# Attention logits on all 128 rows of TensorE, and forget-gate bias tiles by broadcast DMA

## The chip, the cores and the metric

The kernel runs on one core of a Trainium2 chip. A core has five engines with instruction streams of their own: TensorE (PE in the rows of the profile; its weight loads are PEld), VectorE (DVE), ScalarE (ACT), GpSimd (POOL) and SyncE (SP), which here only issues DMAs. The metric is the device time of one execution in microseconds, lower is better; the median of three runs is given.

## The reference

Two transformer blocks in float32, over 1024 tokens of width 1024. Block 1 has a token mixer with 16 heads of 64 (8 heads with a forget gate, 8 with a band of earlier chunks) and a convolutional feed-forward; block 2 has gated linear attention and a squared-relu feed-forward. The change touches only the logits of block 1's two kinds of attention:

```python
# forget heads: cum = running sum of log f
logits = einsum('bhqd,bhkd->bhqk', qb, k) * d**-0.5        # d = 64
logits = logits + cb[..., :, None] - cum[..., None, :]
logits = where(k_pos <= q_pos, logits, -inf)
# band heads: own chunk of 64 and the 8 chunks before it
logits = einsum('bhcqd,bhckd->bhcqk', qc, k_band) * d**-0.5 + bias
p = softmax(logits);  out = p @ v
```

The part of the forget bias that is the same for a whole row of queries, `cb`, cancels in the softmax, so the kernel adds one value per key.

## The kernel before

A float32 value is held as two `float32r` parts, a rounded high one and the rest, low. A product of two such numbers is the sum of high x high, high x low and low x high, accumulated in one PSUM bank; `mm3` (lines 130 to 132) does that in three matmuls with 128 contracted rows.

A head has 64 features, so the high and the low part of one head's queries fit into the 128 rows together. For each pair of heads `k_out` and `q_out` write, from the PSUM result of the projection: `X0`, with the high part of head 0's queries in rows 0 to 63 and the low part (with the other sign) in rows 64 to 127; `X1`, the same for head 1 with the halves exchanged; `Y0` and `Y1`, the keys with the parts the other way round, so that one matmul over 128 rows gives high x low plus low x high; and `Dk`, the high parts of the keys of both heads, 64 rows each. `stage_qk` then takes two matmuls for a strip of up to 512 keys: line 373 with `X` and `Y` on 128 rows, and line 375 with the 64 rows of `X` and `Dk` that hold the high parts. In the forget heads a third one (line 377, bf16) puts the causal mask on the last 128 columns. VectorE adds the bias tile and takes the row's extreme (line 378), ScalarE the exponential (381), VectorE the reciprocal (382), GpSimd the scaling (383). TensorE transposes the result (line 90, `ptp`), it is split in two parts (`ph` on ScalarE, `pl` on VectorE), and line 427 multiplies them with the values.

The bias tile of a forget head (heads 8 to 15) is made by `make_bias`: two matmuls (line 343) with 64 rows of the running sums `cums` against a selector, and two copies by ScalarE (line 344). The bias of a band head comes by DMA (line 346) and is changed by GpSimd.

The attention phase merges several streams: the attention itself (logits run AHEAD = 3 query tiles before the rest), the projections of the next pair of heads or of the values, the modulation products `ada` (loads of `ada_w` on SP, sums on GpSimd), and near the end the loading of earlier results. A scheduler then fixes the order on every engine before the kernel runs; each engine works strictly in that order, and SP issues its DMAs in order too, each one waiting for its source and for its destination to be free. Pairs of heads have their `X` and `Y` tiles in two buffers, logits have two PSUM banks (`S`), bias tiles two buffers.

Of the kernel before, what the change touches and what calls it, by code (L numbers as in the profile page):

```python
# [14 lines left out]
ALU = mybir.AluOpType  # L15
# [28 lines left out]
def merge(gens):  # L44
    """Interleaves streams by their shares of tensor-engine time: gens is a list of (gen, total)."""
    live = [[g, float(total), 0.0] for g, total in gens]
    while live:
        s = min(live, key=lambda e: e[2] / e[1])
        try:
            s[2] += next(s[0]) or 1.0  # L50
        except StopIteration:
            live.remove(s)


def build(tc, I, out, dbg=None, stop=None):
# [13 lines left out]
    def set_banks(st, n, plan):  # L69
        """PSUM of a phase: tag -> (bank count of a tile, buffers, purposes)."""  # L70
        banks.clear()
        for tag, (width, bufs, uses) in plan.items():
            pl = pool(st, f"ps{n}{tag}", bufs, space=PSUM)
            for u in uses.split():
                banks.setdefault(u, deque()).append((pl, tag, 512 * width))
# [6 lines left out]
    def exp_tables(after):  # L82
        """ScalarE's set with both Exp and Ln, once no other one is wanted."""
        with tc.issue_after(after.ins):
            ACT.preload_act_table_set("natural_log_exp_and_others")

# [28 lines left out]
    def w_get(ap, n=P):  # L115
        """Weights loaded and split, in two pieces: the parts of each row block of n columns."""
        m = ap.shape[-1] // 2
        out = []
        for i in range(2):
            r = rawp.tile([P, m], F32, tag="raw", name="raw")  # L120
            SP.dma_start(out=r, in_=ap[:, i * m:i * m + m])
            h = wp.tile([P, m], F32R, tag="wh", name="wh")
            l = wp.tile([P, m], F32R, tag="wl", name="wl")
            split(r, h, l)
            out += [(h[:, c:c + n], l[:, c:c + n]) for c in range(0, m, n)]
        return out

    def mm3(o, ah, al, bh, bl, first, last):
        """o += a^T b of operands in parts: all products but the one below float32's last bit."""
        PE.matmul(out=o, lhsT=ah, rhs=bh, start=first, stop=False)  # L130
        PE.matmul(out=o, lhsT=ah, rhs=bl, start=False, stop=False)  # L131
        PE.matmul(out=o, lhsT=al, rhs=bh, start=False, stop=last)  # L132
# [11 lines left out]
    def ada(v, c0, n, ar, ac):  # L144
        """Columns c0 to c0 + n of modulation vector v: products with the columns of ada_w, summed over rows by VectorE, over partitions by TensorE."""
# [37 lines left out]
    # =====================================================================  # L183
    # block 1: the token mixer
    # =====================================================================
    ydram = [tc.dram_tile([P, T], F32, name=f"ydram{p}") for p in range(8 if stop == "attn" else 7)]

    def attention_phase():
# [25 lines left out]
        def k_out(p, half, psum):  # L214
            Y0, Y1, Dk = pair[p][2:]
            c = slice(half * 512, half * 512 + 512)
            a, b = slice(0, 64), slice(64, 128)
            ACT.copy(Dk[:, c], psum)
            ACT.copy(Y0[b, c], psum[a])
            ACT.copy(Y1[a, c], psum[b])  # L220
            DVE.tensor_tensor(out=Y0[a, c], in0=psum[a], in1=Dk[a, c], op=ALU.subtract)
            DVE.tensor_tensor(out=Y1[b, c], in0=psum[b], in1=Dk[b, c], op=ALU.subtract)

        def alloc_pair(p):
            pair[p] = [qkp.tile([P, T], F32R, tag=n, name=n) for n in ("X0", "X1", "Y0", "Y1", "Dk")]
# [38 lines left out]
        def weights(n, half):  # L264
            """Half of the first pair's weights, in the place of the values to come."""
            r = rawp.tile([P, 512], F32, tag="raw", name="raw")
            h, l = (vp.tile([P, 512], F32R, tag=f"v{4 * n + 2 * half + i}", name="w0") for i in range(2))
            SP.dma_start(out=r, in_=Wqk[n][:, half * 512:half * 512 + 512])
            split(r, h, l)
            wqk[n].append((h, l))  # L270
# [30 lines left out]
        sel8 = f1.tile([64, 8], F32R, name="sel8")  # L301
        selt = f1.tile([64, 8], F32, name="selt")
        DVE.tensor_copy(out=selt, in_=ident[0:64, 0:8])
        DVE.tensor_copy(out=selt[32:64], in_=ident[32:64, 32:40])
        DVE.tensor_copy(out=sel8, in_=selt)
# [5 lines left out]
        cums = f1.tile([64, T], F32R, name="cums")  # L311

        def forget_sums():
            """The forget gates' running sums, in parts."""
            fa = pp.tile([P, T], F32, tag="P", name="fa")[0:8]
            fb = pp.tile([P, T], F32, tag="P", name="fb")[0:8]
            POOL.memset(cums.bitcast(F32), 0.0)
# [13 lines left out]
            ACT.copy(cums[0:8], fa)  # L331
            DVE.tensor_tensor(out=cums[32:40], in0=fa, in1=cums[0:8], op=ALU.subtract)

# [1 line left out]
        bias = {}  # L335

        def make_bias(h):
            bt = bp.tile([P, T], F32, tag="bias", name="bias")
            if h >= 8:
                for half in range(2):  # L340
                    c = slice(half * 512, half * 512 + 512)
                    psum = acc("S")
                    PE.matmul(out=psum, lhsT=sel8[:, h - 8:h - 7].to_broadcast([64, P]), rhs=cums[:, c], start=True, stop=True)
                    ACT.copy(bt[:, c], psum)
# [13 lines left out]
        def stage_qk(h, j, i):  # L358
            t = 2 * j + i
            X0, X1, Y0, Y1, Dk = pair[h // 2]  # L360
            X, Y = (X0, Y0) if h % 2 == 0 else (X1, Y1)
            rows = slice(0, 64) if h % 2 == 0 else slice(64, 128)
# [7 lines left out]
            for n, (c0, c1) in enumerate(zip(cuts, cuts[1:])):  # L370
# [4 lines left out]
                PE.matmul(out=S, lhsT=X[rows, tq], rhs=Dk[rows, kc], start=False, stop=not diag)  # L375
# [89 lines left out]
        def ahead(n):  # L465
            """The logits of the first n query tiles; a negative yield before those of a new pair."""
# [108 lines left out]
    def rstd_of(v, eps, scale=1.0):  # L575
        """(scale * v + eps) ** -0.5 for [P, 1]."""
# [8 lines left out]
    def layer_norm(r, mv, g, b, junk, eng=None):  # L585
        """r: a row's values; mv[:, 0:2]: the sums of its halves."""
# [7 lines left out]
    def add_sum(o, a, b, s):  # L594
        """o = a + b, s its sum over the row."""
        DVE.tensor_tensor_reduce(out=o, in0=a, in1=b, scale=1.0, scalar=0.0, op0=ALU.add, op1=ALU.add, accum_out=s)  # L596
# [6 lines left out]
    def transposed(src, t, hi_t=None, lo_t=None, full=None, scale=None, shift=None, use="xtp"):  # L603
        """[128 tokens, 1024] -> columns of the split transposed activations, with a scale and a shift by feature."""
# [25 lines left out]
    def square_product(wname, wo, done, scale=None, ks=range(KD)):  # L630
        """tokens x 1024 = (transposed activations)^T @ weights, by halves of the columns and token tiles."""
# [35 lines left out]
    def low_rank(hs, ht, c0, n):  # L667
        """[tokens, 32] of n tokens -> their columns of the gates' right factor, in parts."""
# [8 lines left out]
    def gates(hs, h, c0, n, e, with_q):  # L677
        """Per direction, of one head and n tokens: decays to and from the middle of each 128-token tile, and over its two chunks."""
# [35 lines left out]
    def tile_factors(e, nt):  # L714
        """The factor from one tile's state to the next one's, in the order of the direction."""
# [26 lines left out]
    def k_tokens(kts, bufs=None):  # L742
        """[dk, 128 tokens] each -> [128 tokens, dk] side by side."""
# [8 lines left out]
    def context(st):  # L752
        """The states that the context leaves, by head and direction."""
# [21 lines left out]
        def states(h, ek, v, e):  # L775
            """The two directions' states: the keys of the two tiles with the decays that follow them, times the values."""
            kts = []
            for d in range(2):
                a = d
                # the decay over the last chunks, and from the first tile to the second, by direction  # L780
# [80 lines left out]
    # =====================================================================  # L861
    # block 1: the convolutional feed-forward; block 2's modulation beside it
    # =====================================================================
# [40 lines left out]
    def ffn():  # L904
# [57 lines left out]
        def first_values():  # L962
            """The first head's values, and the gates' low-rank products."""
# [58 lines left out]
    # =====================================================================  # L1022
    # block 2: gated linear attention
    # =====================================================================
# [39 lines left out]
    def scan(h):  # L1064
# [17 lines left out]
        def step(d, t, s, tag):  # L1082
            """The state entering the next tile of this direction, with that tile's first decay."""
# [82 lines left out]
    # =====================================================================  # L1166
    # block 2: the squared-relu feed-forward
    # =====================================================================
# [58 lines left out]
def tiles_of(w, cols):  # L1227
    """[d, cols] with d = k * 128 + p as rows p of (k, col)."""
# [11 lines left out]
def by_part(v):  # L1240
    """A vector of 1024 features as [128, 8]."""
# [3 lines left out]
def cut(w):  # L1245
    """[n * 128, 1024] as [n, 2, 128, 512]."""
# [70 lines left out]
```

## Time and profile before

| | before |
|---|---|
| median of 3 runs | 2671.27 us (2670.43 to 2673.04) |
| profiled execution: span from first to last instruction | 2669.8 us; no time of its own beside the span is listed |
| mean granted TensorE clock | 0.993 |
| busy over the span: TensorE, VectorE, ScalarE, GpSimd | 98%, 52%, 38%, 17% |
| attention phase, where the change lies | about 35 to 567 us of the span |
| DMA | 184.93 MB, mean 69 GB/s |

Ends of matmuls are modelled, so a busy TensorE is not one at its peak: how fast it goes is read from the distance between the starts of neighbouring matmuls. In rows of the timeline, two numbers stand first, the start and the duration in us, then the engine, the line, the operation with output<-inputs, rows*columns of the array that are active, and the shape of the moving operand. A bracket at the end says how long the engine idled before and what ended it; "issue" means nothing that the profile shows.

### The profile page before, as it was taken

Reading aid. Unit: us, or ns where it says so; the run is one execution under the profiler, and the core shown is the slowest. Engines: PE = TensorE matmul, PEld = TensorE weight load, DVE = VectorE, ACT = ScalarE, POOL = GpSimd, SP = SyncE. Lnnn points to the kernel's source line nnn. Section 1 sums busy time; section 2 is a strip of 40 time slices with the busy share of each in tenths; the row PEclk is TensorE's granted clock in tenths of the full one; section 3 lists DMA queues with packets and bytes.
Section 4 is the critical chain, followed back from the end, with each engine's and each line's share of the span. In section 5 each row is a group of like instructions: output and inputs, shape, how many; then the busy total and the mean of one; then the engine's idle time right before and its main releaser. Section 6 shows DMA issues by size and latency. Waiting matters only on the chain.

```text
span 2669.8 us, 35397 instructions
## 1 busy us (share of the span) xinstructions
PE 2619.0 (98%) x13322; PEld 2187.1 (82%) x13322; DVE 1396.4 (52%) x2681; ACT 1011.3 (38%) x1909; POOL 445.2 (17%) x598
## 2 busy tenths in 40 slices
PE   8999999999999999999999899999999999999998
PEld 7787877778878888888887788899878888888887
DVE  5756556466755554554556766434442333333365
ACT  5555555564532222222224744333263222222223
POOL 4565632333200000000003400000020000000031
PEclk9999999999999999999999999999999999999999
DMA  4222110142322222222221210102331111111122
GB/s 152 71 61 71 46 51 23 57 156 72 108 86 71 89 63 73 82 64 70 91 79 65 72 38 22 41 28 96 117 104 48 51 48 48 48 48 48 48 83 79
DMA packets 113819, 184.93 MB, mean 69 GB/s; under 512 B 13936, under 2 KB 46320, under 8 KB 113648
## 3 DMA queue, kind: packets, MB, share of 16 engines
q1 hardware_dynamic: 113648, 182.68, 21.5%
q8 instruction: 104, 1.70, 0.3%
q14 instruction: 67, 0.55, 0.1%
HBM read 164.28 MB, written 18.35 MB: 68 GB/s over the span
## 4 chain that ended last, share of the span: by engine, by line
PE 63%; issue 30%; POOL 3%; DVE 2%; ACT 1%; DMA 1%; POOLq 0%; DVEq 0%; SPq 0%; ACTq 0%
PE down L130 4%; PE down L131 4%; PE down L132 4%; PE up L131 4%; PE up L130 4%; PE up L132 4%; PE proj L130 3%; PE proj L132 3%; PE proj L131 3%; PE y L427 3%; PE S L375 2%; PE ptp L90 2%; PE tokp L131 2%; PE tokp L130 2%; PE tokp L132 2%
## 5 line engine op out<-in xcount | busy, mean ns | idle before, releaser
L130 PE MATMUL up<-act_hi,wh 128*128 128x512 f32 x1216 | 475.2, 391 | 6.8 <-DVE conv L922 2.5
L131 PE MATMUL up<-act_lo,wh 128*128 128x512 f32 x1216 | 475.9, 391 | 0.2 <-DVE act_lo L624 0.2
L132 PE MATMUL up<-act_hi,wl 128*128 128x512 f32 x1216 | 474.5, 390 | 0.0
L102 ACT CAST wh<-raw 128x512 fp32r<-128x512 f32 (+2 forms) x268 | 166.3, 624 | 554.7 <-PE up L131 501.2
L103 DVE TENSOR_TENSOR wl<-raw,wh 128x512 fp32r<-128x512 f32 (+2 forms) x268 | 202.4, 761 | 281.4 <-ACT wh L102 268.6
L130 PE MATMUL down<-wdh,gh 128*128 128x512 f32 x864 | 337.6, 391 | 1.1 <-DVE mv L596 0.7
L131 PE MATMUL down<-wdl,gh 128*128 128x512 f32 x864 | 336.9, 390 | 0.3 <-DVE wdl L103 0.2
L132 PE MATMUL down<-wdh,gl 128*128 128x512 f32 x864 | 331.5, 390 | 0.2 <-DVE gl L103 0.2
L130 PEld LDWEIGHTS up<-act_hi,wh 128*128 128x128 f32 x1216 | 228.6, 188 | 55.5 <-ACT conv L920 2.9
L131 PEld LDWEIGHTS up<-act_lo,wh 128*128 128x128 f32 x1216 | 228.8, 188 | 48.0 <-DVE act_lo L624 1.0
L132 PEld LDWEIGHTS up<-act_hi,wl 128*128 128x128 f32 x1216 | 228.8, 188 | 47.3
L579 POOL TENSOR_TENSOR rstd<-rstd,mhalf 128x1 f32<-128x1 f32 x74 | 49.8, 673 | 1241.9 <-DVE rstd L578 1226.6
L102 ACT CAST wdh<-wdraw 128x512 fp32r<-128x512 f32 x108 | 67.1, 622 | 378.6 <-PE down L132 283.3
L1191 DVE TENSOR_TENSOR res<-res,down 128x512 f32<-128x512 f32 x160 | 107.3, 686 | 171.9 <-PE down L132 171.6
L130 PEld LDWEIGHTS down<-wdh,gh 128*128 128x128 f32 x864 | 162.3, 188 | 36.8 <-DVE mv L596 2.2
L131 PEld LDWEIGHTS down<-wdl,gh 128*128 128x128 f32 x864 | 162.3, 188 | 34.5 <-DVE wdl L103 1.3
L132 PEld LDWEIGHTS down<-wdh,gl 128*128 128x128 f32 x864 | 162.2, 188 | 34.2 <-DVE gl L103 0.6
L130 PE MATMUL tokp<-wh,act_hi 128*128 128x256 f32 (+1 forms) x512 | 150.2, 295 | 0.0
L131 PE MATMUL tokp<-wl,act_hi 128*128 128x256 f32 (+1 forms) x512 | 149.7, 293 | 0.0
L132 PE MATMUL tokp<-wh,act_lo 128*128 128x256 f32 (+1 forms) x512 | 148.6, 291 | 0.0
L383 POOL TENSOR_SCALAR P<-P,mx 128x640 f32<-128x640 f32 (+7 forms) x128 | 96.7, 757 | 255.1 <-DVE mx L382 210.5
L381 ACT ACTIVATE P<-P,mx 128x640 f32<-128x640 f32 (+7 forms) x128 | 94.5, 738 | 96.2 <-DVE mx L378 88.5
(302 smaller groups left out, 5205.5 us busy)
## 6 DMA issues: line engine op xcount, KB each, us to landing
ada_w<-in_ada_w SPq DMA_DIRECT2D x192, 128.0 KB, 2.1
raw<-in_w_up SPq DMA_DIRECT2D x88, 256.0 KB, 2.6
raw<-in_mlp_w SPq DMA_DIRECT2D x64, 256.0 KB, 2.6
wdraw<-in_mlp_w SPq DMA_DIRECT2D x64, 256.0 KB, 2.8
wdraw<-in_w_down SPq DMA_DIRECT2D x44, 256.0 KB, 2.6
raw<-in_wqk SPq DMA_DIRECT2D x32, 256.0 KB, 2.8
raw<-in_g_qk SPq DMA_DIRECT2D x24, 256.0 KB, 2.6
raw<-in_g_v SPq DMA_DIRECT2D x24, 256.0 KB, 2.7
```

The lines of the kernel that those rows point to most:

```text
L90: PE.transpose(out=o, in_=a, identity=ident)
L102: ACT.copy(h, raw)
L103: DVE.tensor_tensor(out=l, in0=raw, in1=h, op=ALU.subtract)
L130: PE.matmul(out=o, lhsT=ah, rhs=bh, start=first, stop=False)
L131: PE.matmul(out=o, lhsT=ah, rhs=bl, start=False, stop=False)
L132: PE.matmul(out=o, lhsT=al, rhs=bh, start=False, stop=last)
L375: PE.matmul(out=S, lhsT=X[rows, tq], rhs=Dk[rows, kc], start=False, stop=not diag)
L381: ACT.activation(Pm[:, 0:W], Pm[:, 0:W], AF.Exp, bias=mx[:, 0:1], scale=-1.0, accum_out=mx[:, 1:2])
L383: POOL.tensor_scalar(out=Pm[:, 0:W], in0=Pm[:, 0:W], scalar1=mx[:, 2:3], scalar2=0.0, op0=ALU.mult, op1=ALU.add)
L427: PE.matmul(out=o, lhsT=lhsT, rhs=part[:, off:off + w], start=(first and n == 0 and m == 0), stop=(last and n == len(cur) - 1 and m == 1))
L579: POOL.tensor_tensor(out=t[:, 1:2], in0=t[:, 0:1], in1=mhalf, op=ALU.pow)
L1191: DVE.tensor_tensor(out=r, in0=r, in1=psum, op=ALU.add)
```

## The change

The 64-row matmul with `Dk` becomes one with 128 rows. `Dk` goes, and each head gets a tile `Z` with its keys' high part where `X` has the queries' high part, and the low part where `X` has the low one. So `X` with `Z` gives high x high plus low x low. ScalarE writes the high parts and VectorE the low parts only into the half of the rows where the PSUM result has them; four DMAs for each half of the columns copy them to the other half of the rows, into the other tile (`Y` from `Z`, `Z` from `Y`; 64 rows of 512 values, 128 KB, each). For the bias, the running sums are stored to memory once (`cumd`), and the bias tile of a forget head is one DMA that reads one row of it for all 128 partitions (512 KB); the selector, `cums`, the 16 matmuls and 16 copies go.

```diff
 def k_out(p, half, psum):
-    Y0, Y1, Dk = pair[p][2:]
+    Y0, Y1, Z0, Z1 = pair[p][2:]
     ...
-    ACT.copy(Dk[:, c], psum)
-    ACT.copy(Y0[b, c], psum[a])
-    ACT.copy(Y1[a, c], psum[b])
-    DVE.tensor_tensor(out=Y0[a, c], in0=psum[a], in1=Dk[a, c], op=ALU.subtract)
-    DVE.tensor_tensor(out=Y1[b, c], in0=psum[b], in1=Dk[b, c], op=ALU.subtract)
+    ACT.copy(Z0[a, c], psum[a])
+    ACT.copy(Z1[b, c], psum[b])
+    DVE.tensor_tensor(out=Y0[a, c], in0=psum[a], in1=Z0[a, c], op=ALU.subtract)
+    DVE.tensor_tensor(out=Y1[b, c], in0=psum[b], in1=Z1[b, c], op=ALU.subtract)
+    for o, i, to, of in ((Y0, Z0, b, a), (Y1, Z1, a, b), (Z0, Y0, b, a), (Z1, Y1, a, b)):
+        SP.dma_start(out=o[to, c].bitcast(F32), in_=i[of, c].bitcast(F32))
 ...
-    cums = f1.tile([64, T], F32R, name="cums")
+    cumd = tc.dram_tile([8, T], F32, name="cumd")
 def forget_sums():
-    POOL.memset(cums.bitcast(F32), 0.0)
     ...
-    ACT.copy(cums[0:8], fa)
-    DVE.tensor_tensor(out=cums[32:40], in0=fa, in1=cums[0:8], op=ALU.subtract)
+    SP.dma_start(out=cumd, in_=fa)
 def make_bias(h):
     if h >= 8:
-        for half in range(2):
-            c = slice(half * 512, half * 512 + 512)
-            psum = acc("S")
-            PE.matmul(out=psum, lhsT=sel8[:, h - 8:h - 7].to_broadcast([64, P]), rhs=cums[:, c], start=True, stop=True)
-            ACT.copy(bt[:, c], psum)
+        SP.dma_start(out=bt, in_=cumd[h - 8:h - 7, :].to_broadcast([P, T]))
 def stage_qk(h, j, i):
-    X0, X1, Y0, Y1, Dk = pair[h // 2]
-    X, Y = (X0, Y0) if h % 2 == 0 else (X1, Y1)
-    rows = slice(0, 64) if h % 2 == 0 else slice(64, 128)
+    X, Y, Z = pair[h // 2][h % 2::2]
     ...
     PE.matmul(out=S, lhsT=X[:, tq], rhs=Y[:, kc], start=True, stop=False)
-    PE.matmul(out=S, lhsT=X[rows, tq], rhs=Dk[rows, kc], start=False, stop=not diag)
+    PE.matmul(out=S, lhsT=X[:, tq], rhs=Z[:, kc], start=False, stop=not diag)
```

The scheduler orders the phase anew. The first place is TensorE where the fourth pair of heads (heads 6 and 7) has its first logits; `S` is their PSUM bank, `proj` are projections, `ptp` transposes, `y` products with the values. Before, with lines 373 and 375:

```order
L427 MATMUL y_2789<-ph_2771,v3_2321 128x128
L427 MATMUL y_2789<-pl_2772,v3_2321 128x128
L90 MATMUL ptp_2947<-ident_67,P_2663 128x128
L373 MATMUL S_2907<-Y0_2595,X0_2593 128x128
L375 MATMUL S_2907<-Dk_2597,X0_2593 128x128
L90 MATMUL ptp_2947<-ident_67,P_2702 128x128
L130 MATMUL proj_2931<-act_hi_71,wh_2921 128x512
```

and in the changed kernel, where the two logit matmuls are lines 361 and 363:

```order
L132 MATMUL proj_2880<-act_hi_71,wl_2822 128x512
L361 MATMUL S_2928<-Y0_2609,X0_2607 128x128
L130 MATMUL proj_2953<-act_hi_71,wh_2943 128x512
L131 MATMUL proj_2953<-act_lo_72,wh_2943 128x512
L132 MATMUL proj_2953<-act_hi_71,wl_2944 128x512
L130 MATMUL proj_2953<-act_hi_71,wh_2943 128x512
L131 MATMUL proj_2953<-act_lo_72,wh_2943 128x512
L363 MATMUL S_2928<-Z0_2611,X0_2607 128x128
L132 MATMUL proj_2953<-act_hi_71,wl_2944 128x512
```

The second matmul of the strip, which reads the later of the two copies, stands five projections behind the first.

The second place is SP while the second pair's keys (heads 2 and 3) are made; `ada_w` are loads for the modulation, `raw` weights, `ydram` stores of results. Before:

```order
L151 DMA ada_w_1363<-in_ada_w 128x256
L151 DMA ada_w_1407<-in_ada_w 128x256
L151 DMA ada_w_1526<-in_ada_w 128x256
L121 DMA raw_2139<-in_wv 128x512
L346 DMA bias_1589<-in_relb 128x640
L151 DMA ada_w_1559<-in_ada_w 128x256
```

and in the changed kernel:

```order
L151 DMA ada_w_1371<-in_ada_w 128x256
L223 DMA Y0_902<-Z0_904 64x512
L223 DMA Y1_903<-Z1_905 64x512
L151 DMA ada_w_1415<-in_ada_w 128x256
L223 DMA Z0_904<-Y0_902 64x512
L223 DMA Z1_905<-Y1_903 64x512
L151 DMA ada_w_1534<-in_ada_w 128x256
L121 DMA raw_2153<-in_wv 128x512
L151 DMA ada_w_1567<-in_ada_w 128x256
L223 DMA Y0_902<-Z0_904 64x512
L223 DMA Y1_903<-Z1_905 64x512
```

The copies stand among the loads of `ada_w`, and everything behind them on SP is issued after them.

More of the change, by code (lines that the diff above doesn't have):

```diff
@@ L214, in k_out @@
         def k_out(p, half, psum):
-            Y0, Y1, Dk = pair[p][2:]
+            Y0, Y1, Z0, Z1 = pair[p][2:]
             c = slice(half * 512, half * 512 + 512)
             a, b = slice(0, 64), slice(64, 128)
-            ACT.copy(Dk[:, c], psum)
-            ACT.copy(Y0[b, c], psum[a])
-            ACT.copy(Y1[a, c], psum[b])
-            DVE.tensor_tensor(out=Y0[a, c], in0=psum[a], in1=Dk[a, c], op=ALU.subtract)
-            DVE.tensor_tensor(out=Y1[b, c], in0=psum[b], in1=Dk[b, c], op=ALU.subtract)
+            ACT.copy(Z0[a, c], psum[a])
[4 more added lines that the diff above has]
+                SP.dma_start(out=o[to, c].bitcast(F32), in_=i[of, c].bitcast(F32))
         def alloc_pair(p):
-            pair[p] = [qkp.tile([P, T], F32R, tag=n, name=n) for n in ("X0", "X1", "Y0", "Y1", "Dk")]
+            pair[p] = [qkp.tile([P, T], F32R, tag=n, name=n) for n in ("X0", "X1", "Y0", "Y1", "Z0", "Z1")]
         def qk_proj(p):
@@ L300, in attention_phase @@
         POOL.memset(ones, 1.0)
[L301 to L305, printed above, removed]
         bf = f1.tile([8, 1], F32, name="bf")
```

## Prediction, made before the changed kernel ran

> **What bounds the kernel now.** I read the page first, then windows over the attention phase, then TensorE's waits there, and then the timeline of TensorE around the two matmuls that change.
>
> ```profile
> PE 2619.0 (98%) x13322; PEld 2187.1 (82%) x13322; DVE 1396.4 (52%) x2681; ACT 1011.3 (38%) x1909; POOL 445.2 (17%) x598
> 35.00:522.00 487.00, 486.50 (x2838) 389.69 (x2836) 290.16 (x786) 259.72 (x580) 228.02 (x360) 1.00 0.17 51
> 522.00:567.00 45.00, 42.52 (x215) 30.51 (x215) 34.24 (x101) 34.67 (x80) 21.34 (x23) 0.89 0.29 93
> PE S L373 <- ACT bias L344: 1.4, 2, 0.7
> PE S L373 <- DVE mx L378: 0.7, 1, 0.7
> PE proj L427 <- DVE pl L414: 0.2, 1, 0.2
> ```
>
> In the two window rows the columns behind the length are the busy time (and count) of PE, PEld, DVE, ACT and POOL, then the granted clock, the DMA engines' share and GB/s. From 35 to 522 us TensorE is busy without a break while VectorE has 290 of 487 us, ScalarE 260, GpSimd 228. The waits of TensorE for other engines in the whole of 35 to 566 us are the three rows below: 2.3 us. So in this phase time is TensorE's own time, and what it does more quickly shortens the phase until another engine holds it. Only the last 45 us are mixed: no projections are left there, VectorE and ScalarE are each at 77% of the stretch.
>
> TensorE busy says nothing about its pace. That is in the starts:
>
> ```profile
> 346.04 0.40 PE L131 MATMUL proj<-act_lo,wh 128*128 128x512 f32 x1
> 346.27 0.40 PE L132 MATMUL proj<-act_hi,wl 128*128 128x512 f32 x1
> 346.60 0.50 PE L375 MATMUL S<-Dk,X 64*128 64x512 f32 x1
> 347.03 0.23 PE L377 MATMUL S<-maskb,identb 128*128 128x128 bf16 x1
> ...
> 347.56 0.28 PE L427 MATMUL y<-pl,v 128*128 128x256 f32 x1
> 347.68 0.28 PE L427 MATMUL y<-ph,v 128*128 128x256 f32 x1
> ...
> 348.58 0.44 PE L375 MATMUL S<-Dk,X 64*128 64x384 f32 x1
> 348.95 0.50 PE L130 MATMUL proj<-act_hi,wh 128*128 128x512 f32 x1
> 349.30 0.40 PE L131 MATMUL proj<-act_lo,wh 128*128 128x512 f32 x1
> ...
> 351.28 0.36 PE L373 MATMUL S<-Y,X 128*128 128x256 f32 x1
> 351.57 0.38 PE L375 MATMUL S<-Dk,X 64*128 64x256 f32 x1
> 351.89 0.23 PE L377 MATMUL S<-maskb,identb 128*128 128x128 bf16 x1
> ```
>
> A 128-row matmul with 512 columns is followed by the next after 0.23 us, one with 256 after 0.12, so one with 384 should be after 0.17. Into a 64-row matmul it is 0.33 instead of 0.23 and 0.29 instead of 0.12: 0.10 to 0.17 us lost. Out of one it is 0.43 for 0.23, 0.37 for 0.17, 0.32 for 0.12: 0.20 us each time. And the first full matmul behind it takes 0.35 for 0.23: another 0.12. The weight loads say why:
>
> ```profile
> 348.06 0.35 PEld L90 LDWEIGHTS ptp<-ident,P 128*128 128x128 f32 x3
> 348.58 0.18 PEld L375 LDWEIGHTS S<-Dk,X 64*128 64x128 f32 x1 [0.17 <-issue]
> 348.95 0.19 PEld L130 LDWEIGHTS proj<-act_hi,wh 128*128 128x128 f32 x1 [0.19 <-issue]
> 349.06 0.19 PEld L131 LDWEIGHTS proj<-act_lo,wh 128*128 128x128 f32 x1
> 349.30 0.19 PEld L132 LDWEIGHTS proj<-act_hi,wl 128*128 128x128 f32 x1
> ```
>
> Ordinarily a load runs one matmul ahead (the load for the matmul of 349.30 starts at 349.06). At a 64-row matmul it starts only with the matmul itself, and the load after it only at 348.95, with an empty gap ahead of each: the array is run empty on the way in and on the way out.
>
> Fewer than 128 rows alone is not the reason:
>
> ```profile
> 1505.25 0.30 PE L132 MATMUL tokp<-wh,act_lo 128*128 128x288 f32 x1
> 1505.38 0.62 PE L685 MATMUL z<-hs,a2s 96*128 96x512 f32 x2
> 1505.84 0.30 PE L130 MATMUL tokp<-wh,act_hi 128*128 128x288 f32 x1
> ```
>
> Two 96-row matmuls of 512 columns take 0.46 us together, 0.23 each, and entering them costs nothing.
>
> **A rule against it.** The Trainium skill, "TensorE: Matmul & The Clock Gate", section "Why this matters for your kernels", says that a single matmul on few rows (K=32) takes the time of one on 128; carried over to 64 rows it would make this exchange worth nothing. "TensorEngine Tiling (Array Packing)", section "Key Properties", says that a change of tiling mode drains TensorE, by which each 64-row matmul among 128-row ones pays twice. The rows at 346 to 351 us side with the second; the first would leave only the bias part of the sum below.
>
> **The change part by part.** How many such places there are:
>
> ```profile
> L375 PE MATMUL S<-Dk,X x192: 321/437/687, 35.8 to 564.7; 64*128 64x384 f32 x80, 64*128 64x256 f32 x56, 64*128 64x512 f32 x40, 64*128 64x128 f32 x16
> L343 PE MATMUL S<-cums,sel x16: 389/497/499, 300.4 to 544.7; 64*128 64x512 f32 x16
> L344 ACT COPY bias<-S 128x512 f32<-128x512 f32 x16 | 9.2, 590 | 1.5 <-PE S L343 1.2
> ```
>
> *TensorE.* Loss per 64-row matmul: 0.10 to 0.17 in, 0.20 out, 0.12 behind, 0.42 to 0.49 in these rows; where another small matmul stands next the third part is less or absent (0.30). I take 0.38, between them. 26 of the 208 lie in the last 45 us: 24 strips of the last two heads (4 query tiles of one strip and 4 of two, each) and the two bias matmuls of the last one. Of the other 182: 182 x 0.38 = 69 us. The 14 bias matmuls among them also go as such, 14 x 0.23 = 3 us. The 192 replaced ones stay, with 128 rows at the ordinary pace. Before 522 us that frees 72 us.
>
> *The last 45 us.* 26 x 0.38 plus 2 x 0.23 is 10 us, but there VectorE and ScalarE are at 77%, and TensorE waits for both. Nothing or all of it could come; I take 6, since the strip's own chain, from its matmul to VectorE, gets shorter by the drain too.
>
> *New waits of TensorE.* With 72 us less, 415 us are left for 290 of VectorE (70%), for ScalarE's 260 less 14 bias copies and as many `Dk` copies of the same 128x512, 28 x 0.59, or 243 (59%), and for GpSimd's 228 (55%). None becomes the bound, but in a fixed order some waits appear. The low bound is 0 (2.3 us in 531 now); the high one is the share of TensorE's idle time in the last stretch, 2.48 of 45 or 5.5%, on 415: 23 us. With projections in between it is nearer to the first: I charge 8.
>
> *The copies.* Eight pairs, two halves, four DMAs: 64 of 128 KB, and 8 bias DMAs of 512 KB: 12.6 MB over some 460 us, 27 GB/s on top of 51 to 93, at a DMA share of 0.17 to 0.29. Bandwidth is no matter; delay may be. The pair with little room is the fourth:
>
> ```profile
> 235.08 0.68 DVE L221 TENSOR_TENSOR Y<-proj,Dk 64x512 fp32r<-64x512 f32 x1 [0.89 <-ACT Y L220]
> 239.63 0.30 PE L373 MATMUL S<-Y,X 128*128 128x128 f32 x1
> 234.22 0.33 SPq L346 DMA_DIRECT2D bias<-in_relb  x1
> ada_w<-in_ada_w SPq DMA_DIRECT2D x192, 128.0 KB, 2.1
> 237.80 3.04 SPq L121 DMA_DIRECT2D raw<-in_wv  x2
> 279.96 0.28 PE L130 MATMUL proj<-wh,act_hi 128*128 128x256 f32 x1
> ```
>
> VectorE has the low part at 235.76; the issue of the copy (0.33, and as much for one ahead of it) and 2.1 us for 128 KB give 238.5, and the first logits are at 239.63. With the 4.5 us from the first row to these logits running a sixth quicker (72 of 487), the room is about nothing. The high part, which the first matmul needs, comes one step earlier, and the second one stands five projections (1.1 us) later in the new order. So each pair waits between 0 and about 3 us (all of issue and landing); I charge 2 for all eight, mostly for the first pair and this one.
>
> *SP.* The copies wait for ScalarE and VectorE, and weights, `ada_w` and stores queue behind them. The values' weights of the last two rows are issued at 237.80 and the projections that need them follow from 279.96 on: with such a lead I cost a delay of a few us at nothing; without it, projections would start late by the same 2 to 3 us.
>
> *ScalarE, VectorE, GpSimd.* 17 us less on ScalarE, a memset, a cast and small copies elsewhere: hidden beside TensorE, nothing. The bias by DMA takes away TensorE's two waits for `bias` (1.4 us); with two buffers its tile is free a head ahead, and the store of the sums precedes it by many heads: nothing.
>
> *Sum.* 72 + 6 - 8 - 2 = 68 us off the span of 2669.8. The median of the runs is 1.5 us above that span; 2671.3 - 68 gives 2603.
>
> **The rivals.**
> 1. *The time comes back as waits.* The same drains go, but TensorE, a sixth quicker, meets the softmax chain: the 23 us above, the copies at 3 us for each of 8 pairs (24 us), and nothing in the last stretch: 72 - 23 - 24 = 25 to 55 us of gain, 2616 to 2646. For it: the last stretch, where waits already appear; against it: VectorE at 60%, and 2.3 us of waits now.
> 2. *Rows don't matter.* The loss is due to the second accumulation or to `Dk`, and stays. Then only the bias matmuls go, 16 x (0.23 + 0.38) or 10 us, less 2: 2663. Against it: line 427 accumulates pairs in one bank at 0.12 us a step, and line 343, without accumulation, has the same 64 rows and, by its row, the same median (497 ns for 512 columns, as the 0.50 of line 375).
> 3. *Slower: SP holds the copies.* SP works in order, and `ada_w` and stores stand ahead of copies and between them:
>
> ```profile
> SPq L151 <- POOL ada_acc L155: 17.8, 6, 9.4
> SPq L439 <- DVE mx L378: 32.8, 5, 12.4
> ```
>
> If a wait as the longest in these rows, 9.4 or 12.4 us, fell on each pair's copies, TensorE would stand about 10 us eight times, 80 against 78 freed less 8: 2681. It decides from 8.8 us a pair (70 / 8). Against it: the other 32 waits behind `ada_prod` are short, and the order puts the copies where TensorE's own earlier work has released what stands ahead.
> 4. *More than forecast.* No new waits, and the half clock in the last stretch (0.89 granted, 5 us of 45) goes too: 72 + 10 + 5 = 87, 2584.
>
> **How the numbers follow.** Forecast (55 to 82 us of gain, 2589 to 2616): 0.70. Rival 1: 0.17. Rival 2: 0.04. Rival 3: 0.04. Rival 4: 0.05. The time is that of the first, 2603. The range, 2588 to 2638, holds the first and three quarters of rival 1: about 0.83. About 0.2% (5 us) is what a measurement of this kernel tells from no change. Faster by more: 0.70 + 0.17 + 0.05 and most of rival 2, 0.94; slower 0.04; the same 0.02.
>
> **What would show it.** Starts of 64-row logits and bias matmuls gone; line 363 followed after 0.23 (512) or 0.12 us (256); no empty gap in PEld around it; the attention phase ending near 500 us and all behind it as before. DMA copies landing about 2.1 us after issue, and TensorE waiting for them little at the first logits of a pair. Wrong would be: waits of TensorE for copies over 3 us a pair, or over 25 us in all for `P`, `ph` and `pl`; or line 363 with the same 0.2 us loss on 128 rows.

## The result, and the profile after

The changed kernel takes 2599.11 us (median of 4 runs, 2598.08 to 2599.61), the kernel before 2672.15 us beside it: ratio 0.973, 95% interval 0.9716 to 0.9744. The forecast was 2603, range 2588 to 2638. Medians here and below are of fast executions; one of the five of the run with 64 rows again took 5182.92 us and is left out.

The page's first part, and two windows that cut the attention phase at the first logits of the last two heads:

```profile
span 2597.9 us, 35527 instructions
PE 2543.7 (98%) x13306; PEld 2172.6 (84%) x13306; DVE 1386.3 (53%) x2677; ACT 991.2 (38%) x1876; POOL 440.1 (17%) x597
...
35.00:456.40 421.40, 418.45 (x2800) 377.76 (x2800) 284.24 (x781) 239.31 (x545) 222.28 (x356) 1.00 0.30 86
456.40:507.40 51.00, 41.54 (x271) 33.28 (x270) 43.02 (x118) 43.11 (x96) 25.74 (x28) 0.97 0.46 145
```

TensorE is still busy 98%; its busy time fell by 75 us with nearly the same count of matmuls. In the long window VectorE has 67% and ScalarE 57%, in the last one TensorE only 81% against 84% and 85%.

The timeline around the second logit matmul, now line 363, and the weight loads at the same place:

```profile
319.32 0.33 PE L361 MATMUL S<-Y,X 128*128 128x384 f32 x1
319.49 0.34 PE L363 MATMUL S<-Z,X 128*128 128x384 f32 x1
319.67 0.23 PE L365 MATMUL S<-maskb,identb 128*128 128x128 bf16 x1
...
321.29 0.39 PE L132 MATMUL proj<-act_hi,wl 128*128 128x512 f32 x1
321.52 0.40 PE L361 MATMUL S<-Y,X 128*128 128x512 f32 x1
321.75 0.39 PE L363 MATMUL S<-Z,X 128*128 128x512 f32 x1
321.98 0.28 PE L415 MATMUL y<-ph,v 128*128 128x256 f32 x1
```

```profile
321.29 0.19 PEld L361 LDWEIGHTS S<-Y,X 128*128 128x128 f32 x1
321.52 0.19 PEld L363 LDWEIGHTS S<-Z,X 128*128 128x128 f32 x1
321.76 0.19 PEld L415 LDWEIGHTS y<-ph,v 128*128 128x128 f32 x1
```

Into it 0.23 us, out of it 0.23 (512 columns) or 0.18 (384), where it was 0.33 and 0.43 or 0.37. Each load starts one matmul ahead again, with no gap. The waits of TensorE in the phase (from 35 to 505 us), all rows:

```profile
PE y L415 <- DVE pl L402: 1.9, 4, 0.7
PE proj L415 <- DVE pl L402: 1.7, 5, 0.5
PE S L363 <- DMA Z<-Y: 1.7, 1, 1.7
PE y L415 <- DVE ysum L425: 1.6, 1, 1.6
PE proj L415 <- ACT ph L401: 1.3, 1, 1.3
PE ptp L90 <- POOL P L371: 1.3, 3, 0.6
PE S L361 <- DVE mx L366: 1.2, 3, 0.5
PE y L415 <- ACT ph L401: 0.9, 1, 0.9
PE ptp L90 <- DVE pl L402: 0.2, 1, 0.2
```

That is 11.8 us. The 2.3 us of the kernel before were counted to 566 us, but its last product with the values stands at 577.95; counted to 580 us, all its rows are:

```profile
PE S L373 <- ACT bias L344: 1.4, 2, 0.7
PE proj L427 <- DVE pl L414: 1.2, 3, 0.7
PE y L427 <- DVE pl L414: 1.1, 1, 1.1
PE ptp L90 <- POOL P L383: 0.7, 1, 0.7
PE S L373 <- DVE mx L378: 0.7, 1, 0.7
PE y L427 <- ACT ph L413: 0.6, 1, 0.6
```

So like is compared with like at 5.7 and 11.8 us. The 5.7 all lie behind the first logits of the last two heads; of the 11.8, the same view cut at 456.4 us has 2.6 before these logits and 9.2 behind. Of the 64 copies one is waited for in this window, at the first pair, and one more for 0.50 us at 34.15, just ahead of it. Where the 72 us came from is read by three rows of each timeline: the first logits of the last two heads, the last product with the values, and the first matmul of the feed-forward. Of the kernel before, then of the changed one:

```profile
522.20 0.33 PE L373 MATMUL S<-Y,X 128*128 128x128 f32 x1 [0.70 <-ACT bias L344]
...
577.95 0.27 PE L427 MATMUL proj<-pl,v 128*128 128x128 f32 x1
...
725.75 0.47 PE L130 MATMUL up<-act_hi,wh 128*128 128x512 f32 x1 [1.50 <-DVE mv L596]
```

```profile
456.43 0.28 PE L361 MATMUL S<-Y,X 128*128 128x128 f32 x1
...
507.14 0.27 PE L415 MATMUL proj<-pl,v 128*128 128x128 f32 x1
...
653.96 0.48 PE L130 MATMUL up<-act_hi,wh 128*128 128x512 f32 x1
```

| stretch | before | after | difference |
|---|---|---|---|
| to the first logits of the last two heads | 522.2 | 456.4 | -65.8 |
| from there to the last product with the values | 55.8 | 50.7 | -5.1 |
| from there to the feed-forward | 147.8 | 146.8 | -1.0 |
| the rest of the span | 1944.1 | 1943.9 | -0.2 |

### The profile page after: what moved, and what is told of

The parts are those of the page before. It is cut to its first block, busy times and chain, and to the rows that moved or that the text cites. A ratio compares the mean times of both kernels' runs of the same rounds, so it can differ in the third digit from the quotient of the medians.

```text
span 2597.9 us, 35527 instructions
## 1 busy us (share of the span) xinstructions
PE 2543.7 (98%) x13306; PEld 2172.6 (84%) x13306; DVE 1386.3 (53%) x2677; ACT 991.2 (38%) x1876; POOL 440.1 (17%) x597
## 4 chain that ended last, share of the span: by engine, by line
PE 59%; issue 31%; DVE 3%; POOL 3%; DMA 2%; ACT 1%; SPq 0%; POOLq 0%; DVEq 0%; ACTq 0%
PE down L130 5%; PE down L131 4%; PE down L132 4%; PE up L131 4%; PE up L130 4%; PE up L132 4%; PE proj L130 3%; PE proj L132 3%; PE proj L131 3%; PE tokp L131 2%; PE tokp L130 2%; PE tokp L132 2%; PE y L415 2%; PE ptp L90 2%; PE sq L131 1%
## 5 line engine op out<-in xcount | busy, mean ns | idle before, releaser
L102 ACT CAST wh<-raw 128x512 fp32r<-128x512 f32 (+2 forms) x268 | 165.8, 623 | 556.5 <-PE up L131 511.5
L131 PEld LDWEIGHTS up<-act_lo,wh 128*128 128x128 f32 x1216 | 229.7, 189 | 48.3 <-DVE act_lo L612 0.9
## 6 DMA issues: line engine op xcount, KB each, us to landing
ada_w<-in_ada_w SPq DMA_DIRECT2D x192, 128.0 KB, 2.1
```

The lines of the kernel that those rows point to most:

```text
L102: ACT.copy(h, raw)
```

## The experiments

Theory: each 64-row matmul among 128-row ones runs TensorE's array empty on the way in and out, and in a phase where TensorE hardly waits that is time. Rivals: the gain comes from the bias tiles, from the copies and the lighter ScalarE, or from something else about the second accumulation.

**One part alone: the bias.** The diff's hunks for `forget_sums` and `make_bias`, in the kernel before; logits stay on `Dk`.

> The kernel before with only the bias part: running sums stored to memory, bias tile of a forget head by one broadcast DMA, logits still on 64 rows of Dk. Theory (each 64-row matmul among 128-row ones costs about 0.38 us beyond its columns): 16 x (0.23 + 0.38) = 10 us, less waits for the tile, so 2661 to 2666. Rival (the time came from the bias, whose matmuls and copies stood in the way of the logits' two PSUM banks): most of the 72 us, 2600 to 2630.

Measured 2660.63 us beside 2671.31, ratio 0.9958 (0.9944 to 0.9973): 10.7 us, at the lower edge of theory. The rival is out. The size fits, though only in part by the way that theory had it, as the run on 128-row bias matmuls below shows.

**The rows alone.** In the kernel before:

```diff
-            rows = slice(0, 64) if h % 2 == 0 else slice(64, 128)
+            rows = slice(0, 128)
```

> The kernel before with one edit: the second logit matmul takes all 128 rows of X and Dk. It then also adds the other head's keys times the low parts, so the logits are others; no copies, no Z, bias as before with its 16 matmuls on 64 rows. Theory: 192 drains less, about 60 to 66 us, 2605 to 2612, 64-row matmuls left on line 343 only. Rival (the loss belongs to the second accumulation or to Dk as an operand, not to the rows): no change, 2670 to 2673. Rival (copies and Z are what helps): no change.

Measured 2608.44 us, ratio 0.9764 (0.9748 to 0.9779): 63 us from one line that moves no work to another engine; 63/192 is 0.33 us a matmul. There is no copy and no `Z` in it. This run and the next compute other logits and serve for the time alone. Part of the 63 us is clock: in the kernel before it is 0.88 over the last 55.75 us of the phase, in this run 0.96 over its last 48.32, some 5 us as an estimate, so the rows alone are worth nearer to 58 us, 0.30 each.

**96 rows.** The same line with `slice(0, 96)`. For the odd heads, whose high parts lie in rows 64 to 127, this leaves out half of the high x high products.

> As the run with 128 rows, but rows 0 to 95 of X and Dk for every head (logits are others again). Theory that a tiling mode of 64 rows is what drains, so that 96 rows run as 128: the same as with 128 rows, 2605 to 2612. Rival, that any change of the row count between neighbours drains: 2668 to 2674. The page's rule that rows do not matter: 2670 to 2673 in both runs.

Measured 2606.54 us, ratio 0.9757 (0.9742 to 0.9772): as with 128. Its timeline:

```profile
322.83 0.39 PE L373 MATMUL S<-Y,X 128*128 128x512 f32 x1
323.06 0.40 PE L375 MATMUL S<-Dk,X 96*128 96x512 f32 x1
323.29 0.28 PE L427 MATMUL y<-ph,v 128*128 128x256 f32 x1
```

0.23 us in and out on 96 rows. So it is not that neighbours differ in their row count; 64 rows is what costs. The Trainium skill's "TensorEngine Tiling (Array Packing)", "Tiling Modes", lists row modes of 128, 64 and 32 only; that 96 rows run without a loss among 128-row matmuls is what these rows add.

**The changed kernel with 64 rows again.**

```diff
-    PE.matmul(out=S, lhsT=X[:, tq], rhs=Z[:, kc], start=False, stop=not diag)
+    PE.matmul(out=S, lhsT=X[rows, tq], rhs=Z[rows, kc], start=False, stop=not diag)
```

with `rows` as in the kernel before.

> The changed kernel with one edit back: the second logit matmul on the 64 rows of X and Z that hold the high parts; copies, Z and bias by DMA stay. Theory: the drains come back, only the bias part (10 us) stays, less some us for copies: 2660 to 2668. Rival (the DMAs and the work taken off ScalarE made it quicker): 2600 to 2615.

Measured 2657.82 us, ratio 0.9961 (0.994 to 0.9981), 2 us below theory's range and not told apart from the bias part alone (0.9944 to 0.9973). So the copies and the lighter ScalarE bring and cost nothing by themselves that these runs can tell; 2657.8 - 2599.1 is 59 us, 0.31 a matmul. The drains are back in its timeline (line 364 here), and the last two rows are its first logits of the last two heads and its last product with the values:

```profile
342.33 0.40 PE L132 MATMUL proj<-act_hi,wl 128*128 128x512 f32 x1
342.66 0.49 PE L364 MATMUL S<-Z,X 64*128 64x512 f32 x1
343.08 0.23 PE L366 MATMUL S<-maskb,identb 128*128 128x128 bf16 x1
...
511.51 0.28 PE L362 MATMUL S<-Y,X 128*128 128x128 f32 x1
...
562.42 0.41 PE L416 MATMUL proj<-pl,v 128*128 128x128 f32 x1
```

Up to the first logits of the last two heads the changed kernel is 511.5 - 456.4 = 55.1 us ahead, at a granted clock of 1.00 in both: 0.33 us for each of the 168 matmuls there. From there to the last product it is 50.9 us with 64 rows and 50.7 without: the 24 drains of the last two heads cost nothing that shows.

**Half the dose.** 64 rows in the odd heads only.

> The changed kernel with the second logit matmul on 64 rows in the odd heads only (96 of 192 strips). Theory (each drain adds its own price to a TensorE that is never waiting): half of the way to the run with all on 64 rows, 2627 to 2631. Rival (drains hide behind waits in part, or cost more when close together): below 2622 or above 2640.

Measured 2626.98 us, ratio 0.9832 (0.9807 to 0.9857): 28 us above the changed kernel for 96 matmuls, 0.29 each, at the lower edge of theory. The price adds up.

**No copies.** In the changed kernel's `k_out`:

```diff
-    for o, i, to, of in (...): SP.dma_start(...)
+    ACT.copy(Y0[b, c], psum[a])
+    ACT.copy(Y1[a, c], psum[b])
+    DVE.tensor_tensor(out=Z0[b, c], in0=psum[a], in1=Z0[a, c], op=ALU.subtract)
+    DVE.tensor_tensor(out=Z1[a, c], in0=psum[b], in1=Z1[b, c], op=ALU.subtract)
```

> The changed kernel with no copies by DMA: ScalarE and VectorE write both halves of Y and Z from PSUM (two casts and two subtractions more for each half of a pair's keys, some 19 us on ScalarE and 22 us on VectorE over the phase). Theory (TensorE's pace is the time, copies cost one wait of 1.7 us at the first pair): 2596 to 2602. Rival (VectorE or ScalarE is near its limit, so the copies by DMA are what lets the gain through): 2605 to 2620.

Measured 2602.13 us, ratio 0.9739 (0.9717 to 0.976), just above the upper edge of what theory said and not told apart from the changed kernel's 0.973. So the DMA form is not what lets the gain through; that it is better by a few us is not excluded.

**The first pair without copies.** The same lines for `p == 0` only, run beside the kernel before, and again beside the changed kernel on the same chip.

> The changed kernel, but the first pair's copies by ScalarE and VectorE, all others by DMA. Theory: the 1.7 us wait of TensorE at the first strips goes and nothing else: 2597 to 2599. Rival (the wait is only moved, since the first pair's softmax is late anyway): 2599 to 2602.

> The changed kernel with the first pair's copies by ScalarE and VectorE, beside the changed kernel on the same chip. Theory: 1 to 3 us below it. Rival: the same.

> The changed kernel itself, beside the last two on the same chip: 2597 to 2601.

Measured 2596.44 us at first (0.9719, 0.9697 to 0.9741), below both ranges; beside the changed kernel 2598.22 against 2598.02 (0.9732 and 0.9731). The same: the 1 to 3 us of the first time were not there. The wait is only moved, as the rival said. Rows of TensorE of the changed kernel as it ran beside this one, then of this one:

```profile
36.07 0.47 PE L361 MATMUL S<-Y,X 128*128 128x128 f32 x2 [0.99 <-DMA Y<-Z]
```

```profile
37.69 0.36 PE L130 MATMUL proj<-wh,act_hi 128*128 128x264 f32 x1 [1.61 <-DVE X L212]
```

With two more subtractions per half, VectorE frees the projections' PSUM bank later: TensorE's waits for it (`X`, L212) are 3.1 us between 28 and 46 us, and 1.4 us in the changed kernel.

**All drains out, nothing else.** In the kernel before the logits on all rows of `Dk`, and `sel8`, `cums` with 128 rows, zero behind the first 64.

> The kernel before with all its 64-row matmuls of the phase on 128 rows and nothing else: the logits on all rows of X and Dk (which adds the other head's keys times the low parts), the bias matmuls on 128 rows of zero-padded sums. No DMA is added and none of the 16 bias matmuls or copies goes. Theory: 6 us below the run with the logits alone on 128 rows (16 x 0.38), 2600 to 2604; the rest to the changed kernel is the 16 matmuls' own 3.7 us. Rival (the bias is costly by its PSUM banks and copies, not its drains): the same as that run, 2607 to 2610.

Measured 2606.43 us, ratio 0.9756 (0.9732 to 0.978). This missed: it lies between theory and rival, its interval overlaps that of the run with the logits alone (0.9748 to 0.9779), and 16 drains were to bring 6 us, not 2. So the bias matmuls were taken by themselves:

**The bias matmuls on 128 rows alone.**

```diff
-        sel8 = f1.tile([64, 8], F32R, name="sel8")
+        sel8 = f1.tile([P, 8], F32R, name="sel8")
         ...
-        cums = f1.tile([64, T], F32R, name="cums")
+        cums = f1.tile([P, T], F32R, name="cums")
         ...
-                    PE.matmul(out=psum, lhsT=sel8[:, h - 8:h - 7].to_broadcast([64, P]), rhs=cums[:, c], start=True, stop=True)
+                    PE.matmul(out=psum, lhsT=sel8[:, h - 8:h - 7].to_broadcast([P, P]), rhs=cums[:, c], start=True, stop=True)
```

> The kernel before with its 16 bias matmuls on 128 rows of zero-padded sums and nothing else: 64-row logits stay, so do the bias matmuls' columns and copies. Theory (drains add up, the rest of the bias part is the matmuls' own columns): 16 x 0.31 to 0.38 = 5 to 6 us, 2665 to 2667, and the bias part alone (2661) is 4 us further. Rival (the bias part gains by the half-clock stretches around the last bias tiles that its trace no longer has, 17 us of half clock in the trace before, none in that one): 2669 to 2672 with half clock left, or near 2661 without.

Measured 2668.95 us, ratio 0.9997 (0.9987 to 1.0006): no change that can be told, and at the rival's lower edge. Its timeline shows more than its time; the first logits of the last two heads and the last product with the values:

```profile
519.54 0.33 PE L373 MATMUL S<-Y,X 128*128 128x128 f32 x1 [1.42 <-ACT bias L344]
...
574.94 0.28 PE L427 MATMUL proj<-pl,v 128*128 128x128 f32 x1
```

The kernel before has 522.20 and 577.95, so the phase is 3.0 us shorter: the 16 drains of the bias are there, at 0.19 us each, below the 0.31 to 0.38 of theory. Behind the last product, where the edit changes nothing, this execution takes 3.2 us longer. Its 12 executions have a mean granted clock of 0.9916, the 17 of the kernel before beside them 0.9927; 0.0011 of 2670 us is 3 us, by which a like gain is hidden in the times (an estimate).

The half clock at the last pair stays, as the rival said. Windows over some 24 us from the first logits of the last two heads on: of the kernel before, of this run, and of the run with the bias part alone.

```profile
522.00:546.00 24.00, 22.37 (x99) 16.02 (x100) 14.72 (x46) 17.13 (x39) 14.32 (x15) 0.79 0.24 78
```

```profile
519.50:543.40 23.90, 22.39 (x102) 16.27 (x102) 14.57 (x46) 17.07 (x38) 14.18 (x15) 0.79 0.24 78
```

```profile
510.80:534.80 24.00, 22.64 (x138) 16.45 (x136) 19.25 (x58) 21.05 (x49) 19.09 (x20) 1.00 0.42 131
```

In the first two the granted clock is 0.79, and in the third it is 1.00 and TensorE gets 138 matmuls done instead of 99 and 102. What stands ahead of the slow stretch, in the kernel before:

```profile
523.69 0.45 PE L373 MATMUL S<-Y,X 128*128 128x256 f32 x1 [0.75 <-ACT bias L344]
523.93 0.41 PE L427 MATMUL y<-ph,v 128*128 128x256 f32 x1
524.14 0.42 PE L427 MATMUL y<-pl,v 128*128 128x256 f32 x1
...
523.90:530.70 6.80, 6.80 (x27) 5.33 (x26) 2.81 (x10) 5.38 (x15) 4.93 (x7) 0.50 0.48 162
```

The bias tile of the last pair's first head is made in the logits' PSUM banks by ScalarE's copies, TensorE waits for them, and then runs at half clock for 6.8 us (a step of 0.21 instead of 0.12 for 256 columns). A tile that comes by DMA takes this wait away, and this half clock is gone with it. But such a wait does not by itself bring the clock down each time. The run with the logits on 128 rows has the same two waits, longer ones, and behind them the clock is 1.00:

```profile
PE S L373 <- ACT bias L344: 2.0, 2, 1.0
463.80:487.80 24.00, 21.88 (x152) 17.98 (x152) 20.08 (x64) 22.73 (x55) 17.98 (x20) 1.00 0.37 118
```

And the kernel before is at 0.52 from 128.0 to 131.5 us, where TensorE waits for nothing. In these four traces the half clock stands at the start of the last pair where both the waits and the 64-row logits are there, and not where one of them is missing; what sets the clock stays open.

With the bias part alone the last product stands at 562.04, 15.9 us earlier than before. The 16 matmuls' columns (16 x 0.23 = 3.7), their drains (3.0) and half of the 17 us at half clock (8.5), none of which is left in this trace, would make 15.2 of it. This is an estimate from one execution of each; the medians differ by 10.7.

## Why the prediction was right, point by point

- *TensorE's pace bounds the phase, and a 64-row matmul drains the array twice.* Shown: one line in the kernel before brings 63 us, the same line put back into the changed kernel takes 59 away, and half of it 28. Rival 2 (rows don't matter) is out. That the array runs empty is read from the late weight loads; no row shows the array itself. The Trainium skill, "TensorE: Matmul & The Clock Gate", "Why this matters for your kernels", has a single matmul on few rows (K=32) as costing the same. For 64-row matmuls that stand among 128-row ones the 63 us decide against carrying that over.
- *0.38 us each.* Too high. Before the last stretch it is 0.33 for the logits (55.1 us for 168) and 0.19 for the bias, in the last stretch nothing that shows, so 0.29 to 0.33 over all 192. The 182 drains that the forecast put at 69 us come to 58.
- *3 us for the bias matmuls' columns, their 16 drains at 0.38.* The columns are as said, the drains mis-sized: 3.0 us by the trace of the run on 128-row bias matmuls, not 6. The bias part alone still brings 10.7 us as against 10; the rest goes, by the clocks above, with the half clock, which the forecast had only in rival 4.
- *6 us in the last stretch.* 5.1 by the table, but not by the reason given, that the drains shorten the strip's chain: with 64 rows back in the changed kernel the stretch is 0.2 us longer. In the kernel before its clock was 0.88, in the changed one 0.97, which is worth about 5 us of the stretch (an estimate). Either part alone also shortens it, to 51.3 us (bias) and 48.3 (rows). That the number was met is luck.
- *8 us of new waits, 2 for the copies.* Before the last stretch, where the forecast charged these 10 us, the waits grew from 0 to 2.6 us, of which copies have 1.7, in one place, the first pair. The other growth, from 5.7 to 9.2, is in the last stretch.

The copies' times:

```profile
Y<-Z SPq DMA_DIRECT2D x32, 128.0 KB, 2.3
Z<-Y SPq DMA_DIRECT2D x32, 128.0 KB, 2.3
bias<-cumd SPq DMA_DIRECT2D x8, 512.0 KB, 3.8
```

- 2.3 us to landing, against 2.1 taken from the loads of the same size. The fourth pair's logits, at no room in the forecast, waited for nothing.
- *Slower by SP holding the copies (rival 3), or time returned as waits (rival 1).* Neither: 11.8 us of waits, not 23 and 24.
- *Nothing behind the phase changes.* The last two rows of the table: -1.0 and -0.2 us.
- *The sum, 68 us for 73.* The mechanism is right, but that the number came so near is in part luck: drains some 11 us too high and waits some 7 too high took each other away. Before the last stretch, drains (58), bias columns (3) and the half clock near 130 us (2) less 2.6 of waits make 60 of the 65.8 us measured; the rest stays open.

## What to carry to other kernels

Look at the distance between starts of neighbouring matmuls, not at TensorE's busy time: in a phase at 100% busy, 208 matmuls lost 0.2 to 0.3 us each, except in the last stretch. Where a 64-row matmul has to stand alone among 128-row ones, fill it to 128 rows, if only with products that are zero or small, or to 96, when operands allow; that was worth 0.3 us a place here, though twice as many rows take part, and nothing where TensorE was no longer the bound. The copies to other partitions by DMA landed 2.3 us after their issue, and TensorE waited for them only at the first pair, whose logits follow at once.

## What the runs showed of the hardware that was not expected

That 96 rows take no drain was expected from the rows at 1505 us. The clock was not: the granted clock went to half for 6.8 us right behind two waits of TensorE of 0.70 and 0.75 us, and to 0.52 from 128.0 to 131.5 us where it waited for nothing. The first of these stretches recurred at the same place in the run with 128-row bias matmuls (0.79 over 24 us). It was gone where the bias came by DMA, and also where the logits ran on 128 rows, behind two waits of about 1 us each.
